# Moving the look at w2, the w2 slices and the third and fourth range of w1 in the plan of a two-layer GELU block

## The chip, the core and the metric

The kernel runs on one core of a Trainium2 chip. The metric is the device time in microseconds (us) of an execution. Engines are named as in the profile: PE (TensorE, the matrix products), PEld (its weight loads), DVE (VectorE), ACT (ScalarE), POOL (GpSimd) and SP (SyncE, which issues most transfers). Transfers between DRAM and the core go through 16 DMA engines.

## The reference

```
x: (8, 1024, 1024)   w1: (1024, 4096)   w2: (4096, 1024)      all float32
h = x @ w1
h = 0.5 * h * (1 + tanh(sqrt(2 / pi) * (h + 0.044715 * h ** 3)))
out = h @ w2
```

## The kernel before

All products run in float16 with float32 sums; x, w1 and w2 are scaled by their largest entries first. Both products are done by block schemes with fewer products than the plain one, whose left and right factors are sums of blocks that DVE makes beforehand.

**First product.** The rows of x come in 32 pairs k of two tiles of 128 rows, the columns of w1 in 4 ranges r (each of 512 columns in both halves of w1). One (k, r) is a quad: a Quad1 has seven block products m1 to m7 of four matmuls of 512 columns, in the psum banks pa, pb and pc; the first seven quads are Plain, with 32 matmuls. The list `order` fixes the sequence: the first 6 pairs with range 0, then 1, 2 and 3 (quads 0 to 23), then pairs 6 to 27 with all four ranges each (quads 24 to 111), then the last 4 pairs range by range. A range's factors are prepared while the range ahead of it is multiplied: eight loads (load_w1, L257, on POOL's queue for ranges 1 to 3), eight looks for the largest entry (look_w1, a DVE reduction, L143), widest_w1 (L268, and the `spread` at L148), scale_w1 (a matmul `rows` of 128x128 on PE at L153 that brings the largest to all partitions, read back at L156, with the scales at L273 and L274), eight casts to float16 (cast_w1, L166 on ACT, L168 on POOL, L170 on DVE), and four sums T1 to T4 of 128x2048 (sum_w1, on DVE, L159 and L162). Quad1 needs T2 at m6, T1 at m5, T3 at m7 and T4 at m4; m7 and m4 of a quad run in the next unit, m3 in the one behind that. The sums of x blocks (xs) are on DVE too, in four pieces a pair.

After a quad ACT copies pa (L455, L465, L474), DVE adds pb and pc to the copies (the e groups of L159), ACT takes the gelu (L406), POOL scales and casts (g, L168), and SP stores g to DRAM (gd, L411).

**w2.** While the middle quads run, w2 is read twice. The look: 32 tiles of 128x1024 (look_w2_load, L298, on SP), one reduction each on DVE (look_w2, the w2c group at L143), then widest_w2 and scale_w2. Then eight slices c: four loads (load_w2, L322, on SP), four casts (cast_w2, the wu groups, two on DVE at L170 and two on POOL at L168), 32 sums of 128x256 on DVE (sum_w2, wt), and stores of the sums to DRAM (wd, L344 and L347). In the last 16 quads they are fetched from there (L353).

**What sets the order.** It is written by hand: `plan(u, slot, f, ...)` puts a call into one of seven slots 0 to 6 of unit u, and `unit` writes the quad's products with `background(u, slot)` between them; `early(p, ...)` is slot p % 4 of unit p // 4. Each engine keeps the order in which the calls are written, so an instruction that waits holds up all that stand behind it on its engine, and a transfer that waits for a buffer all behind it in its queue. Loop `k` of x: load_x, look_x on ACT (junk, L181), cast_x on DVE, turn_x (a transposing transfer, L198, on SP), sum_x.

**Buffers.** wpool has 28 buffers of 4 KB a partition (w1 tiles, w1 factors, at first x tiles); k4 has 15 of the same size (x, xT, xs, look tiles, w2 tiles, wu, wt); a tile takes a free one, and its first writer waits for the last reader of the tile ahead of it.

Of the kernel before, what the change touches and what calls it, by code (L numbers as in the profile page):

```python
# [26 lines left out]
B11, T4, B21, B22, T1, T2, T3 = range(7)  # L27
# [48 lines left out]
def kernel(  # L76
# [18 lines left out]
    IK = I // P // 2  # L95
# [3 lines left out]
    FIRST = 6  # L99
# [6 lines left out]
    k4 = ctx.enter_context(tc.tile_pool(name="k4", bufs=15))  # L106
# [33 lines left out]
    V, S, G = nc.vector, nc.scalar, nc.gpsimd  # L140
# [436 lines left out]
    def plan(u, slot, f, *args):  # L577
        assert 0 <= u, (f, args)
        todo.setdefault((u, slot), []).append((f, args))
# [6 lines left out]
    def early(p, f, *args):  # L586
        plan(p // 4, p % 4, f, *args)

    for k in range(1, FIRST):
        for h in range(2):  # L590
            c = 2 * k + h
# [15 lines left out]
        early((3, 4, 6, 7, 8, 9, 10, 11)[n], load_w1, 1, n)  # L607
        early((7, 8, 10, 11, 12, 13, 14, 15)[n], look_w1, 1, n, True)
    early(15, widest_w1, 1)
    early(17, scale_w1, 1)  # L610
    early(17, factors, 0, FIRST, 1)
    for n in range(8):
        early(17 + n // 2, cast_w1, 1, n, (V, S, G, V, S, V, G, V)[n])
    for i, t in enumerate((T1, T3, T2, T4)):
        plan(*((5, 3), (FIRST, 0), (FIRST, 1), (FIRST + 1, 2))[i], sum_w1, 1, t)
    for r in range(2, NR):
        u = (r - 1) * FIRST
        for n in range(8):
            v = u - 1 + n // 2
            plan(v, 1 if v >= FIRST else 0, load_w1, r, n, *((k4, "k4") if r == 3 and n < 2 else ()))  # L620
            plan(v + 1, 3 + n % 2, look_w1, r, n, True)
        plan(u + 3, 4, widest_w1, r)
        plan(u + 4, 1, scale_w1, r)
        plan(u + 4, 1, factors, 0, FIRST, r)
        for n in range(8):
            v = u + 4 + n // 6
            plan(v, 3 + n % 4 * (n < 6), cast_w1, r, n, S if n % 2 else G)
        for i, t in enumerate((T1, T3, T2, T4)):
            plan(u + 5, 4 + i - i // 3, sum_w1, r, t)
    for i, t in enumerate((T1, T3, T2, T4)):  # L630
        plan(3 * FIRST + i, 5, sum_w1, 0, t)

    for k in list(middle) + list(last):
        a = at[k] if k in middle else at[last[0]]
        for h in range(2):
            c = 2 * k + h
# [9 lines left out]

    u = at[middle[0]] - 1
    for ic in range(2 * IK):
        plan(u + ic - 1, 3, look_w2_load, ic)
        plan(u + ic, 6, look_w2, ic)  # L650
    u += 2 * IK
    plan(u, 4, widest_w2)
    plan(u + 1, 1, scale_w2)
    stored = [max(i for i, o in enumerate(RIGHT_SUMS) if RIGHT_PLACE[o[0] - 16][0] == t) for t in range(3)]
    for c in range(8):
        v = u + 2 + c * 11 // 2
        for j in range(4):
            plan(*((v - 1, 1), (v - 1, 3), (v - 1, 6), (v, 1))[j], load_w2, c, j)
            plan(v, (1, 2, 4, 6)[j], cast_w2, c, j, G if j % 2 else V)
        for i in range(len(RIGHT_SUMS)):  # L660
            plan(*divmod(7 * (v + 1) + i, 7), sum_w2, c, i)
            for t in range(3):
                if i == stored[t]:
                    plan(*divmod(7 * (v + 1) + i + 2, 7), store_w2, c, t)
        for node in FORMS:
            if node < 16:
                plan(v + 2, 3, store_block, c, node)
    assert v + 6 < at[last[0]]
    for i, node in enumerate(FORMS):
        r, n = divmod(i, 7)  # L670
# [46 lines left out]
    with tc.manual_schedule(  # L717
# [14 lines left out]
        for c in range(2):  # L732
# [6 lines left out]
            t = x16[c]  # L739
# [63 lines left out]
```

## Time and profile before

| what | value |
|---|---|
| three runs, us | 1552.01, 1553.94, 1554.4 (median 1553.94) |
| profiled execution, us | 1554.94 |
| its span, us | 1552.9 |
| granted PE clock, mean | 1.0 |
| DMA busy share, 175 to 375 us; 380 to 650 us | 0.78; 0.88 |
| DVE busy, 175 to 375 us; 380 to 650 us | 131.39 us; 213.97 us |
| HBM read, written | 96.99 MB, 114.29 MB |

The profile's times run from the span's start. The page's busy line gives each engine's busy time, its share of the span and its instructions. In a list of waits, a line has who waited, for whom, the sum in us, how often, and the longest. In a timeline a line has start, length, engine, line of the kernel, operation, output and inputs, and in brackets how long the engine had been idle before and what ended that. In the chain of waits a piece has start, length and what it was.

The first product lasts to about 820 us of the span, the second from there to the end. Quad 12, the first with range 2, starts at 104.9 us, quad 18, the first with range 3, at 143.8, quad 24 at 181.4, and quad 57, where the first slice of w2 is cast, at 381.1.

### The profile page before, as it was taken

To read this page: it belongs to the slowest core of one execution; us is meant where nothing else is said; L and a number is where in the kernel's file an instruction comes from. 1 tells how busy PE (TensorE), PEld (TensorE's weight loads), DVE (VectorE), ACT (ScalarE), POOL (GpSimd) and SP (SyncE) were. 2 spreads that over 40 slices of the span, in tenths; PEclk is the share of its full clock that TensorE was granted. 3 is DMA by queue.
4 is the path that set the end of the run, shared out by engine and by line. 5 is a ranking of instruction groups with operands and counts; after the bars stand their busy time and mean duration, and the time that the engine had idled before them with its cause. 6 is when DMAs were issued, how large, how long until landed. Compare 5 with 4: busy or idle time off the path is not lost.

```text
span 1552.9 us, 28548 instructions
## 1 busy us (share of the span) xinstructions
PE 1523.7 (98%) x10415; PEld 1016.2 (65%) x10415; DVE 1176.9 (76%) x2361; ACT 726.0 (47%) x1281; POOL 448.6 (29%) x568
## 2 busy tenths in 40 slices
PE   7989999999999999999999999999999999999999
PEld 4434444444444444444447888888888888888888
DVE  6886666666788886765238888888888888888886
ACT  6567777777777777787662111111111111111111
POOL 2667544445565665554442000000000000000000
PEclk9999999999999999999999999999999999999999
DMA  8555778787897988983699677677668667776872
GB/s 322 179 175 185 207 232 256 219 253 209 256 275 234 277 257 238 278 241 116 195 249 263 121 151 140 137 132 159 130 125 158 141 134 135 154 135 120 164 140 79
DMA packets 459804, 293.91 MB, mean 189 GB/s; under 512 B 333840, under 2 KB 427024, under 8 KB 459664
## 3 DMA queue, kind: packets, MB, share of 16 engines
q1 hardware_dynamic: 456208, 279.52, 70.8%
q0 software_dynamic: 3456, 12.58, 2.5%
q8 instruction: 81, 1.33, 0.4%
q14 instruction: 59, 0.48, 0.1%
HBM read 96.99 MB, written 114.29 MB: 136 GB/s over the span
## 4 chain that ended last, share of the span: by engine, by line
PE 91%; DMA 3%; ACT 2%; DVE 2%; issue 1%; POOL 1%; SPq 0%; ACTq 0%; POOLq 0%; DVEq 0%
PE pa L359 48%; PE pc L359 29%; PE pb L359 13%; DMA wn<-in_w_dram 1%; DMA gd<-g 1%; ACT e L406 1%; DMA w<-wd 1%; ACT junk L181 1%; POOL g L168 0%; ACT w L166 0%; PE pb L371 0%; DVE w1c L143 0%; DVE e L159 0%; DVE w L162 0%; PE turned L207 0%
## 5 line engine op out<-in xcount | busy, mean ns | idle before, releaser
L168 POOL TENSOR_SCALAR g<-e,rs 128x512 f16<-128x512 f32 x512 | 400.3, 792 | 354.1 <-ACT e L406 279.7
L359 PEld LDWEIGHTS <-gs 128*128 128x128 f16 x4608 | 450.6, 98 | 56.0 <-DVE gs L162 1.6
L359 PEld LDWEIGHTS <-xs 128*128 128x128 f16 x1936 | 189.3, 98 | 238.2 <-issue 8.2
L159 DVE TENSOR_TENSOR e<-pc,e 128x512 f32<-128x512 f32 x242 | 160.7, 684 | 196.0 <-ACT e L474 195.3
L359 PEld LDWEIGHTS <-xT 128*128 128x128 f16 x1676 | 163.5, 98 | 195.2 <-DVE xT L214 0.4
L359 PE MATMUL pa<-w,gs 128*128 128x256 f16 x2304 | 288.3, 273 | 1.6 <-ACT e L406 1.0
L406 ACT ACTIVATE e<-e,us 128x512 f32<-128x512 f32 x363 | 250.6, 720 | 21.1 <-DVE e L159 20.8
L359 PE MATMUL pa<-w,xs 128*128 128x512 f16 x968 | 248.4, 379 | 8.9 <-ACT e L455 5.9
L359 PE MATMUL pa<-w,xT 128*128 128x512 f16 x1080 | 255.6, 379 | 0.2 <-DVE xT L214 0.2
L359 PE MATMUL pc<-w,xs 128*128 128x512 f16 x968 | 248.4, 379 | 0.0
L359 PEld LDWEIGHTS <-gT 128*128 128x128 f16 x2048 | 200.3, 98 | 23.7 <-DMA w<-wd 0.6
L528 ACT ACTIVATE o<-pa,vo 128x256 f32<-128x256 f32 x96 | 45.2, 471 | 336.1 <-PE pa L359 333.4
L359 PE MATMUL pc<-w,gs 128*128 128x256 f16 x1536 | 193.8, 273 | 0.3 <-DMA w<-wd 0.3
L359 PE MATMUL pa<-w,gT 128*128 128x256 f16 x1024 | 132.7, 273 | 0.3 <-DMA w<-wd 0.3
L359 PE MATMUL pb<-w,xT 128*128 128x512 f16 x484 | 124.2, 379 | 0.0
L524 DVE SCALAR_TENSOR_TENSOR o<-pc,vo,o 128x256 f32<-128x256 f32 x160 | 77.0, 481 | 58.7 <-PE pc L359 58.7
L465 ACT COPY e<-pa 128x512 f32<-128x512 f32 x121 | 70.8, 585 | 92.2 <-PE pa L359 88.6
L162 DVE TENSOR_TENSOR gs<-gT,gs 128x1024 f16<-128x1024 f16 x160 | 109.2, 682 | 1.2 <-DMA gT<-gd 0.5
L524 DVE SCALAR_TENSOR_TENSOR o<-pa,vo,o 128x256 f32<-128x256 f32 x192 | 91.9, 479 | 19.4 <-PE pa L359 19.1
L359 PE MATMUL pb<-w,gs 128*128 128x256 f16 x768 | 99.5, 273 | 0.3 <-DVE gs L162 0.3
L359 PE MATMUL pc<-w,gT 128*128 128x256 f16 x768 | 99.5, 273 | 0.0
L455 ACT COPY e<-pa 128x512 f32<-128x512 f32 x121 | 69.8, 577 | 45.8 <-PE pa L359 45.6
(84 smaller groups left out, 1355.7 us busy)
## 6 DMA issues: line engine op xcount, KB each, us to landing
gd<-g SPq DMA_DIRECT2D x484, 128.0 KB, 3.0
wn<-in_w_dram SPq DMA_DIRECT2D x72, 512.0 KB, 5.5
xn<-in_x_dram SPq DMA_DIRECT2D x64, 512.0 KB, 5.7
out_dram<-o SPq DMA_DIRECT2D x62, 512.0 KB, 3.3
w<-wd SPq DMA_DIRECT2D x25, 512.0 KB, 5.9
wn<-in_w_dram POOLq DMA_DIRECT2D x24, 512.0 KB, 5.8
wd<-wt SPq DMA_DIRECT2D x24, 512.0 KB, 4.9
gd<-g SPq DMA_DIRECT2D x14, 256.0 KB, 4.9
```

Source lines behind the costliest of these rows:

```text
L159: V.tensor_tensor(out=o, in0=a, in1=b, op=ALU.add)
L162: V.tensor_tensor(out=o, in0=a, in1=b, op=ALU.subtract)
L168: G.tensor_scalar(out=o, in0=i, scalar1=s, scalar2=1.0, op0=ALU.mult, op1=ALU.mult)
L181: S.activation(out=junk, in_=xraw[c], func=ACT.Abs, accum_out=xl[:, c:c + 1])
L359: nc.tensor.matmul(bank, lhsT=left(i), rhs=right[i], start=start and i == 0, stop=i == n - 1, skip_group_check=True,)
L406: S.activation(out=e, in_=src, func=ACT.Gelu_apprx_tanh, scale=self.u[half])
L455: S.copy(self.e11, self.pa)
L465: S.copy(self.e12, self.pa)
L524: V.scalar_tensor_tensor(out=o, in0=ps, scalar=v, in1=o, op0=ALU.mult, op1=ALU.add)
L528: S.activation(out=o, in_=ps, func=ACT.Copy, scale=v)
```

## The change

- Range 1: scale, factors and casts stand a quarter of a quad later (early 18 and on for 17 and on). T1 to T4 are made in the order T1, T2, T3, T4, at (6,0), (6,2), (7,1), (7,3), where T1, T3, T2, T4 stood at (5,3), (6,0), (6,1), (7,2).
- Ranges 2 and 3 (the third and fourth): u is one less, so all loads, looks, casts and the scale stand a quad sooner; widest stands in slot 5 instead of 4; the sums stand at (u+5, 4), (u+5, 6), (u+6, 1) and (u+6, 3) of the smaller u. All loads stand in slot 1, and the two of range 3 that used pool k4 use wpool.
- The look at w2: one tile every 35/8 slots (8 in 5 quads) instead of one a quad, each loaded 7 slots ahead of its look instead of 10. It ends in quad 42 instead of 54; widest_w2 stands in quad 43 instead of 55.
- The slices of w2: one every 7 quads, from quad 45 to 94, instead of every 5.5 from 57 to 95. The loads of slice v stand at (v-2,4), (v-2,6), (v-1,2), (v-1,4) instead of (v-1,1), (v-1,3), (v-1,6), (v,1); casts, sums and stores stand as before against v.

```diff
-    early(17, scale_w1, 1)
-    early(17, factors, 0, FIRST, 1)
+    early(18, scale_w1, 1)
+    early(18, factors, 0, FIRST, 1)
     for n in range(8):
-        early(17 + n // 2, cast_w1, 1, n, (V, S, G, V, S, V, G, V)[n])
-    for i, t in enumerate((T1, T3, T2, T4)):
-        plan(*((5, 3), (FIRST, 0), (FIRST, 1), (FIRST + 1, 2))[i], sum_w1, 1, t)
+        early(18 + n // 2, cast_w1, 1, n, (V, S, G, V, S, V, G, V)[n])
+    for i, t in enumerate((T1, T2, T3, T4)):
+        plan(FIRST + i // 2, (0, 2, 1, 3)[i], sum_w1, 1, t)
     for r in range(2, NR):
-        u = (r - 1) * FIRST
+        u = (r - 1) * FIRST - 1
         for n in range(8):
             v = u - 1 + n // 2
-            plan(v, 1 if v >= FIRST else 0, load_w1, r, n, *((k4, "k4") if r == 3 and n < 2 else ()))
+            plan(v, 1, load_w1, r, n)
             plan(v + 1, 3 + n % 2, look_w1, r, n, True)
-        plan(u + 3, 4, widest_w1, r)
+        plan(u + 3, 5, widest_w1, r)
         plan(u + 4, 1, scale_w1, r)
...
         for i, t in enumerate((T1, T3, T2, T4)):
-            plan(u + 5, 4 + i - i // 3, sum_w1, r, t)
+            plan(u + 5 + i // 2, (4, 6, 1, 3)[i], sum_w1, r, t)
...
     for ic in range(2 * IK):
-        plan(u + ic - 1, 3, look_w2_load, ic)
-        plan(u + ic, 6, look_w2, ic)
-    u += 2 * IK
+        t = 7 * u + ic * 35 // 8
+        plan(*divmod(t - 7, 7), look_w2_load, ic)
+        plan(*divmod(t, 7), look_w2, ic)
+    u += 20
...
     for c in range(8):
-        v = u + 2 + c * 11 // 2
+        v = u + 2 + c * 7
         for j in range(4):
-            plan(*((v - 1, 1), (v - 1, 3), (v - 1, 6), (v, 1))[j], load_w2, c, j)
+            plan(*((v - 2, 4), (v - 2, 6), (v - 1, 2), (v - 1, 4))[j], load_w2, c, j)
             plan(v, (1, 2, 4, 6)[j], cast_w2, c, j, G if j % 2 else V)
```

## The prediction

> **What bounds the kernel now.** I read the page first, then the waits of TensorE (PE), then the chain and the timelines around the longest of them. A quad below is a unit u, one (k, r) product: 28 products of 512 columns, 6.045 us when nothing waits (the chain repeats every 6.04 us from 150 to 380 us).
>
> ```profile
> PE 1523.7 (98%) x10415; PEld 1016.2 (65%) x10415; DVE 1176.9 (76%) x2361; ACT 726.0 (47%) x1281; POOL 448.6 (29%) x568
> ```
>
> PE is busy for 98%, so only its gaps can be gained, 29 us in all. 11.6 us of them lie in the first 40 us, 3.3 at the end, and 2.4 at 800 to 860 us, where the second product begins; the change touches none of these. The rest stands in three lines of the waits of PE:
>
> ```profile
> PE pa L359 <- ACT e L455: 5.9, 8, 2.0
> PE pa L359 <- DVE w L162: 3.0, 2, 1.8
> PE rows L153 <- DVE spread L148: 2.8, 2, 2.1
> ```
>
> So 11.7 us, with 0.2 us at an xT copy 11.9 us, is all that this change can touch. PE's timeline places it: 0.68 and 0.21 at 56 us (scale of range 1); then range 2 and range 3:
>
> ```profile
> 93.85 0.33 PE L153 MATMUL rows<-identity,spread 128*128 128x128 f32 x1 [2.13 <-DVE spread L148]
> ...
> 102.31 1.02 PE L359 MATMUL pa<-w,xs 128*128 128x512 f16 x4 [0.36 <-ACT e L455]
> ...
> 110.32 1.04 PE L359 MATMUL pa<-w,xs 128*128 128x512 f16 x4 [1.80 <-DVE w L162]
> ```
>
> Range 3 has 0.36 and 1.19 at 141 and 148 us, and no wait at its rows matmul. Between 380 and 650 us (w2's slices) there are six waits, 5.2 us, all for ACT's copy L455. The waits of VectorE (DVE) in that stretch, and the chain at 484 us, tell why:
>
> ```profile
> DVE wu L170 <- DMA wn<-in_w_dram: 20.1, 9, 4.4
> ```
> ```profile
> 484.58 5.49 DMA wn<-in_w_dram
> ...
> 490.10 0.76 DVE wu L170
> ...
> 491.24 0.61 DVE e L159
> ...
> 494.95 1.11 ACT junk L181 x2
> 496.07 0.48 ACT e L455
> ...
> 496.59 1.02 PE pa L359 x4
> ```
>
> A w2 tile lands late, the cast L170 holds up DVE, the add behind it comes late, ACT waits for the add with its gelu, and the copy that frees PE's bank comes last. Waits of DVE of 3.27, 3.65, 3.73 and 4.44 us cost PE 0.3 to 2.05 us; shorter ones cost nothing.
>
> **w2's slices (gain).** No work is removed; 32 loads and 40 stores of SP's queue are moved. Before, a slice's four loads stand 7, 6, 5 and 5 slots ahead of their casts (7 slots a quad, 0.86 us each: 6.0 to 4.3 us), and the landing view gives 4.0/5.8/8.4 us (least, median, most) for line 322. After, they stand 11, 10, 9 and 9 slots ahead, 9.5 to 7.8 us: each gains 3.4 us or more. That covers the 3.27 wholly and leaves 0.3 to 1.0 of the other three, under what PE feels. Slices every 7 quads in place of 5.5 also thin out the 32 sums on DVE (0.2 us each) and 3.6 MB of DMA a slice, which ran at a DMA share of 0.88 from 380 to 650 us. In SP's queue the loads pass the g stores and a transpose; in the changed program's order (counted in PE's products) the buffers they take were last read 10 to 28 us earlier, where before four loads took a buffer freed less than 6 us earlier, so SP stops less. Residue 0.6 (between none and 1.7): **-4.6 us** (-5.2 to -3.5).
>
> **Looks at w2.** 32 looks of 1.14 us (L143), in 20 quads in place of 32: DVE gets 0.7 us more a quad, and its busy time from 175 to 375 us is 131 of 200 us, so that lies beside PE. The load stands 7 slots ahead and not 10, 2.6 us less. Before, looks began 7.7 to 10.5 us after the issue, so now 5.1 to 7.9, against 3.7/4.1/6.9 us to landing: a wait of up to 1.8 us at the worst, below the 3 us from which PE felt one. Queued behind a waiting look are the adds L159, and behind these ACT's gelu and copy. Nearest rows: 0 PE waits from 150 to 380 us. **0** (0 to +1).
>
> **Range 1 of w1, a quarter quad later.** The rows matmul no longer stands ahead of the third product of quad 4, but that product waits for the xT copy (L214, ends 56.8) behind look, spread and copy on DVE, which do not move. So the 0.9 us stays, and the rows matmul (0.2) no longer hides in it. Its sums come just in time: T3 is needed at 79.5 us and is ready at 78.2 by the shortest rows, 79.7 by the long ones. **+0.2** (0 to +0.5).
>
> **Range 2, a quad sooner (the step that I doubt).** 8 loads on POOL's queue (0.75 us each), 8 looks, widest, spread, rows, 8 casts, 4 sums move up. From 63.24 to 93.72 us DVE works without a break (30.4 busy of 30.5 us), and the spread is the end of that work. The changed order of DVE's instructions up to the spread has three xs pieces less (0.34, 0.49, 0.34), three adds of 0.6 less, one cast of 0.69 more: 30.5 - 1.2 - 1.8 + 0.7 = 28.2 us. So the spread is ready at 63.4 + 28.2 = 91.6 us, 2 us sooner; but PE wants it a whole quad sooner, behind m7 of quad 9, at 85.51 + 0.2 = 85.7. **The wait does not go, it grows from 2.13 to as much as 5.9 us.** With each row at its shortest the work of 30.5 us would be 25.4, because sums that take 1.13 us stand in the trace at up to 2.2 where POOL's casts run beside them; by the same rows the new order takes 23.2, and with a third of the drag 25.5, a wait of 3.2. I take 4.6, nearer the middle: +2.5. Then the sums of range 2 (10,4) to (11,3) are a quad ahead of quad 12, and the 1.80 goes: -1.8. ACT's batch of three casts (0.36) moves along unchanged. **+0.7** (-0.7 to +2.0).
>
> The Trainium skill (SBUF — State Buffer, "SBUF: two separate sides") says that VectorE with two SBUF inputs and GpSimd lock a shared port pair for a whole instruction; the trace agrees (the sum of 2048 at 1.13 alone, 2.2 beside POOL's). By that rule alone the drag would follow POOL's casts, which stay, and the wait would be nearer 5.9 than 3.2.
>
> **Range 3, a quad sooner.** Nothing else fills DVE from quad 11 to 14: looks 2.3 and adds 1.9 of 6 us. Its spread stood ready at 132.3 for a rows matmul at 132.77; the relative slots stay. The 1.19 of T2 goes, 0.36 stays. The two tiles that leave pool k4 for wpool take slots freed long before. **-1.2** (-1.55 to -0.8).
>
> **Sum.** -4.6 + 0 + 0.2 + 0.7 - 1.2 = -4.9 us. The profiled execution took 1554.94 us (span 1552.9 and 2.0 around it), so 1550.0; it lies 1.0 above the median of the runs, 1553.94, so **1549.0** against that median. 0.2% (3.1 us) is about what a measurement of this kernel can tell from no change.
>
> **Rivals.**
> *The wall at quad 9 eats the gain.* The wait is 5.9 us (+3.8 instead of +2.5), T3 is late by 0.3, and the clock falls after so long a gap. For the last: the start has a PE gap of 4.53 us, and the 30 warm-up products behind it take 5.58 us, 16 later ones 1.91 (0.11 each): 2.1 us lost. The longest gap later on is 2.13, with the granted clock at 1.00. So +1.3 + 0.3 + 2.1, 1552.7 us. The Trainium skill (TensorE: Matmul & The Clock Gate, "What's actually happening") puts the fall to half clock after an idle window of about 3.4 us; an estimate from that page is a loss of 1.7 us, 1550.7 with nothing else. Within 0.2%; chance 0.18.
> *w2's waits were not the lead.* SP lags by the g stores (the second slice's first load went out 6.6 us after its slot), so an earlier slot gives no earlier issue; half of the 4.6 stays: 1551.3. Against it: POOL's casts, for which SP waits, are themselves behind late w2 tiles. 0.10.
> *Looks become the bound, slower.* The stretch moves 232 GB/s, 1.40 MB a quad; 0.6 looks more make 1.72 MB, at the 277 GB/s of the densest 40 us slice 6.2 us a quad, over 6.045: 20 x 0.17 = 3.4 us. Around each of five x loads (2 of 512 KB) landings then pass the 3 us of slack, 1.6 us each, 8 us: 1560.4. It decides from landings of about 8 us, and only one in the present 32 reached 6.9. 0.10.
>
> **Chances.** Forecast 0.62, rivals 0.18, 0.10, 0.10. The first two rivals fall within 0.2%: faster 0.62, same 0.28, slower 0.10. The range goes from the best ends (-5.2 - 0.7 - 1.5 = -7.4, 1546.5) to the first rival, 1553.0; the last is left out.
>
> **What would show it.** w2: no DVE wait for wn over 2 us from 330 to 650 us, and at most 0.6 us of PE waits there. Looks: w2c from 181 to some 300 us, no PE wait. Range 2: a PE wait for the spread of 3.2 to 5.9 us near 86 us, none for w L162. Range 3: no w L162 wait. Wrong would be a short wait at quad 9 (DVE less bound than I sum up), or PE waits among the looks.

## The result and the profile after

The changed kernel takes 1555.59 us (median of 20 runs, 1552.82 to 1560.09), the kernel before 1553.05 (20 runs, 1550.72 to 1556.36) beside it: ratio 1.0015, 95% interval 1.0008 to 1.0022, or +1.2 to +3.4 us. That is within 0.2%, and on the other side of no change than the forecast of 1549.0; the time lies above the range, which ended at 1553.0. The profiled execution took 1556.61 us (span 1554.8), 1.7 more than the one of before.

The page's busy line of the changed kernel, then four of PE's waits (who waited, for whom, sum, times, longest):

```profile
PE 1525.8 (98%) x10415; PEld 1016.7 (65%) x10415; DVE 1179.2 (76%) x2361; ACT 724.2 (47%) x1281; POOL 456.4 (29%) x568
```
```profile
PE rows L153 <- DVE spread L148: 4.3, 2, 3.9
PE pa L359 <- ACT e L455: 3.7, 5, 1.7
PE pa L359 <- DVE xT L214: 1.1, 1, 1.1
...
PE pa L359 <- ACT xT L212: 0.9, 1, 0.9
```

The waits that the change aimed at are smaller: 3.7 us for L455 where there were 5.9, and none for w L162. But PE is busy for 2.1 us *more* with the same 10415 instructions: they ran slower. The timeline of PE around quad 9 and the windows there (us, busy time of PE, PEld, DVE, ACT, POOL, then granted clock, DMA share, GB/s) show where:

```profile
85.47 1.03 PE L359 MATMUL pa<-w,xs 128*128 128x512 f16 x4
90.42 0.48 PE L153 MATMUL rows<-identity,spread 128*128 128x128 f32 x1 [3.92 <-DVE spread L148]
90.69 1.91 PE L359 MATMUL pc<-w,xs 128*128 128x512 f16 x4
92.39 1.91 PE L359 MATMUL pb<-w,xT 128*128 128x512 f16 x4
94.10 1.91 PE L359 MATMUL pa<-w,xs 128*128 128x512 f16 x4
95.81 1.09 PE L359 MATMUL pc<-w,xs 128*128 128x512 f16 x4
```
```profile
88.00:90.00 2.00, 0.00 (x0) 0.00 (x0) 2.00 (x5) 0.66 (x2) 1.56 (x2) 0.77 0.24 81
90.00:92.00 2.00, 1.58 (x5) 0.70 (x6) 1.78 (x8) 0.00 (x0) 0.30 (x1) 0.50 0.34 116
...
94.00:96.00 2.00, 2.00 (x6) 0.76 (x5) 1.81 (x5) 0.00 (x0) 0.00 (x0) 0.52 0.00 0
96.00:98.00 2.00, 2.00 (x11) 0.88 (x9) 0.11 (x1) 1.89 (x4) 0.60 (x1) 1.00 0.00 0
```

Range 2's rows matmul now stands at quad 9 and waits 3.92 us (forecast 4.6, bounds 3.2 to 5.9). Behind it the clock is at half until 96 us: three groups of four products take 1.91 us in place of 1.03. That is some 2.6 us, nearly the 2.1 of the first rival, and not in the forecast.

Two other things are new. At the sums of range 2 a wait of 1.07 us (at 114.9 us) stands where 1.80 stood. And among the looks, which had cost PE nothing, there is one of 1.69 us at 256 us and one of 0.37 at 310. The timeline of the changed kernel there, first SP's queue, then the engines:

```profile
241.76 2.78 SPq L198 DMA_TRANSPOSE xT<-x  x1
244.64 1.21 SPq L411 DMA_DIRECT2D gd<-g  x2
245.91 1.50 SPq L298 DMA_DIRECT2D wn<-in_w_dram  x1
```
```profile
252.29 1.22 DVE L143 TENSOR_REDUCE w2c<-wn 128x1 f32<-128x1024 f32 x1 [3.92 <-DMA wn<-in_w_dram]
...
254.14 0.72 ACT L406 ACTIVATE e<-e,us 128x512 f32<-128x512 f32 x1 [3.29 <-DVE e L159]
254.77 1.04 ACT L181 ACTIVATE junk<-xn 128x1024 bf16<-128x1024 f32 x1
...
255.81 0.56 ACT L455 COPY e<-pa 128x512 f32<-128x512 f32 x1
...
256.43 1.02 PE L359 MATMUL pa<-w,xs 128*128 128x512 f16 x4 [1.69 <-ACT e L455]
```

The issue of a transpose holds SP for 2.78 us (the median of its 52 issues is 1.24), the look's load goes out behind it, VectorE stands 3.92 us at the look, ACT's gelu waits for the add behind the look, and PE for the copy that stands behind the gelu and ACT's look at x (L181). It is the chain that the forecast had read at the slices, now at the looks. Of the six gaps of 5.2 us at the slices none is left. By this one execution: slices -5.2, range 3 -1.2, looks +2.1, range 1 +1.1, range 2 +1.1 and the clock +2.6, the start of the second product (waits for transfers of w) +1.4; together +1.9, and the span grew by 1.9.

### The profile page after: what moved, and what is told of

It reads as the page before. It is cut to its first block, busy times and chain, and to the rows that moved or that the text cites. A ratio compares the mean times of both kernels' runs of the same rounds, so it can differ in the third digit from the quotient of the medians.

```text
span 1554.8 us, 28528 instructions
## 1 busy us (share of the span) xinstructions
PE 1525.8 (98%) x10415; PEld 1016.7 (65%) x10415; DVE 1179.2 (76%) x2361; ACT 724.2 (47%) x1281; POOL 456.4 (29%) x568
## 3 DMA queue, kind: packets, MB, share of 16 engines
q8 instruction: 81, 1.33, 0.3%
## 4 chain that ended last, share of the span: by engine, by line
PE 92%; DMA 3%; DVE 3%; ACT 1%; issue 1%; POOL 1%; SPq 0%; ACTq 0%; DVEq 0%; POOLq 0%
PE pa L359 49%; PE pc L359 29%; PE pb L359 13%; DMA gd<-g 1%; DMA w<-wd 1%; DMA wn<-in_w_dram 1%; DVE w1c L143 1%; DVE e L159 0%; PE pb L371 0%; DVE w L162 0%; POOL g L168 0%; DVE xs L162 0%; ACT e L406 0%; PE turned L207 0%; ACT junk L181 0%
## 5 line engine op out<-in xcount | busy, mean ns | idle before, releaser
L168 POOL TENSOR_SCALAR g<-e,rs 128x512 f16<-128x512 f32 x512 | 405.5, 803 | 368.3 <-ACT e L406 290.8
L162 DVE TENSOR_TENSOR gs<-gT,gs 128x1024 f16<-128x1024 f16 x160 | 109.7, 686 | 1.0 <-POOL g L168 0.5
L524 DVE SCALAR_TENSOR_TENSOR o<-pa,vo,o 128x256 f32<-128x256 f32 x192 | 92.1, 480 | 20.3 <-PE pa L359 20.1
L455 ACT COPY e<-pa 128x512 f32<-128x512 f32 x121 | 69.8, 577 | 48.3 <-PE pa L359 47.5
```

The costliest lines, as they stand in the source:

```text
L162: V.tensor_tensor(out=o, in0=a, in1=b, op=ALU.subtract)
L168: G.tensor_scalar(out=o, in0=i, scalar1=s, scalar2=1.0, op0=ALU.mult, op1=ALU.mult)
L455: S.copy(self.e11, self.pa)
L524: V.scalar_tensor_tensor(out=o, in0=ps, scalar=v, in1=o, op0=ALU.mult, op1=ALU.add)
```

## The experiments

Ratios are to the kernel before, measured between the runs of each (5 in e11, 8 to 12 in the others); "us" is the ratio less 1, times the median of the kernel before, good to about 1.6 us either way, so a difference of two of them to about 2. "Clock" is the mean granted clock over a kernel's timed runs (in the kernel before 0.9994 to 0.9996); 0.001 of it is 1.55 us. The single executions agree: in the 188 of these kernels and the changed one, an execution took 1.5 us longer for each 0.001 that its clock lay lower than in others of the same kernel (standard error 0.14).

| run | what | ratio, 95% | us | clock |
|---|---|---|---|---|
| e1 | w1 part alone | 0.9997, 0.9986 to 1.0009 | -0.5 | 0.9984 |
| e2 | w2 part alone | 0.9996, 0.9986 to 1.0006 | -0.6 | 0.9993 |
| e3 | range 2 back | 1.0009, 0.9999 to 1.0020 | +1.4 | 0.9981 |
| e4 | ranges 1 and 2 back | 1.0014, 1.0003 to 1.0025 | +2.2 | 0.9982 |
| e5 | w2 part, looks loaded sooner | 0.9974, 0.9965 to 0.9983 | -4.0 | 0.9995 |
| e6 | changed, idle products | 1.0017, 1.0006 to 1.0027 | +2.6 | 0.9993 |
| e7 | changed, half looks at range 2 | 0.9987, 0.9974 to 0.9999 | -2.0 | 0.9994 |
| e8 | changed, looks loaded sooner | 0.9992, 0.9982 to 1.0001 | -1.2 | 0.9985 |
| e9 | e8 with idle products | 0.9975, 0.9965 to 0.9986 | -3.9 | 0.9998 |
| e10 | e5, slices' loads at the old lead | 0.9986, 0.9975 to 0.9996 | -2.2 | 0.9993 |
| e11 | e5, one cast moved to VectorE | 0.9947, 0.9935 to 0.9959 | -8.2 | 0.9996 |
| e12 | looks alone, loaded sooner | 0.9998, 0.9987 to 1.0009 | -0.3 | 0.9987 |
| f1 | e8 again | 0.9986, 0.9976 to 0.9995 | -2.2 | 0.9986 |
| f2 | e9 again | 0.9976, 0.9967 to 0.9985 | -3.7 | 0.9996 |
| f3 | e8, half the idle products | 0.9969, 0.9959 to 0.9979 | -4.8 | 0.9998 |
| f4 | e6 again | 1.0017, 1.0007 to 1.0026 | +2.6 | 0.9994 |

The first four shared one chip, e5 to e8 a second, e9 to e12 a third, f1 to f4 the second again.

### The parts by themselves: e1 to e4

e1, against the changed kernel:

```diff
-        t = 7 * u + ic * 35 // 8
-        plan(*divmod(t - 7, 7), look_w2_load, ic)
-        plan(*divmod(t, 7), look_w2, ic)
-    u += 20
+        plan(u + ic - 1, 3, look_w2_load, ic)
+        plan(u + ic, 6, look_w2, ic)
+    u += 2 * IK
...
-        v = u + 2 + c * 7
+        v = u + 2 + c * 11 // 2
...
-            plan(*((v - 2, 4), (v - 2, 6), (v - 1, 2), (v - 1, 4))[j], load_w2, c, j)
+            plan(*((v - 1, 1), (v - 1, 3), (v - 1, 6), (v, 1))[j], load_w2, c, j)
```

> The changed kernel with its w2 part (looks and slices) as in the kernel before: only ranges 1 to 3 of w1 are moved. Theory A (the price lies in range 2: PE waits 3.9 us for the spread at quad 9, the granted clock falls to 0.50 for some 6 us behind it, which costs 2.6 us, and a new wait of 1.07 us comes at quad 13; range 1 costs 1.1, range 3 gains 1.2): +3.6 us against the kernel before, with the gap at 86 us and the fallen clock at 90 to 96 us in its profile. Theory B (w2's denser looks and the start of the second product cost what w2's slices gain; the w1 part is what I forecast, -0.3): between -1 and +1 us.

e2 is the kernel before with these lines the other way round.

> The changed kernel with its w1 part as in the kernel before: only w2's looks and slices are moved. Theory A: the six gaps of 5.2 us among the slices go, the looks give one wait of up to 2 us: -3 to -5 us against the kernel before, no granted clock below 0.9 near 90 us. Theory B: +1 to +2.5 us, as the changed kernel.

e3 and e4, against the changed kernel: range 2 gets the loop body that the kernel before has, range 3 keeps the new one; in e4 range 1 has the old lines too.

```diff
-    for r in range(2, NR):
-        u = (r - 1) * FIRST - 1
+    for r in range(2, 3):
+        u = (r - 1) * FIRST
...
+    for r in range(3, 4):
+        u = (r - 1) * FIRST - 1
```

> The changed kernel with range 2 alone back at the slots it has in the kernel before. Theory A: the wait for the spread is 2.1 us again and not 3.9, the clock stays at 1.00 there, the 1.8 us wait for T2 comes back: 3.7 us under the changed kernel, so -1 to -3 us against the kernel before. Theory B: no more than 1 us under the changed kernel.

> As the run before it, with range 1 back as well; range 3 and w2 stay changed. Theory A: a further 1.1 us (the two waits of 0.86 and 1.15 us at 52 and 58 us become 0.9 again), so -3 to -4.5 us against the kernel before, the fastest of the four. Theory B: as the run before it, within 0.5 us, since range 1's wait is for an xT copy that does not move.

Neither theory stands. e1 has the gap of 3.92 us and the fallen clock in its profile, as theory A said, but a time of -0.5 and not +3.6. e2 gained 0.6 where A said 3 to 5, though the gaps at the slices are gone from its profile; it has 2.10 and 0.37 us at the looks. And e3 and e4 did not get the price back. PE's waits in e4 tell why, with VectorE's timeline in e3:

```profile
PE pa L359 <- DVE w L162: 4.0, 1, 4.0
```
```profile
103.40 1.21 DVE L143 TENSOR_REDUCE w1c<-wn 128x1 f32<-128x1024 f32 x1
104.53 1.57 DVE L162 TENSOR_TENSOR w<-w 128x2048 f16<-128x2048 f16 x1
106.03 1.21 DVE L143 TENSOR_REDUCE w1c<-wn 128x1 f32<-128x1024 f32 x1
107.16 5.69 DVE L162 TENSOR_TENSOR w<-w 128x2048 f16<-128x2048 f16 x3
```

With range 2 back, two looks at range 3 (w1c), a quad sooner, stand between its sums (w, L162) on VectorE: PE's wait for T2 goes from 1.80 to 4.0 us. The moves of the two ranges hang together, so these runs put one long gap in the place of another and could not price range 2. The clock's records are instructive. The gap of 4.0 us is followed by half clock in e4 (0.50 from 112 to 118 us) and by full clock in e3; a gap of 2.13 us, the same as in the kernel before, is followed by half clock in e4:

```profile
92.00:94.00 2.00, 0.63 (x4) 0.39 (x5) 1.93 (x5) 1.06 (x2) 1.46 (x2) 1.00 0.00 1
94.00:96.00 2.00, 2.00 (x8) 0.81 (x7) 1.93 (x8) 0.00 (x0) 1.96 (x4) 0.67 0.50 141
96.00:98.00 2.00, 2.00 (x7) 0.66 (x5) 2.00 (x1) 0.19 (x1) 1.81 (x2) 0.50 0.87 291
```

So the same gap brings a fall in one execution and none in another (the section on the clock shows when), and the mean clock of the timed runs says more than one profile.

### The looks: e5 and e8

The loads of the looks move 4 slots up, in e5 in the kernel e2, in e8 in the changed kernel:

```diff
-        plan(*divmod(t - 7, 7), look_w2_load, ic)
+        plan(*divmod(t - 11, 7), look_w2_load, ic)
```

> The w2 part alone (w1 as in the kernel before), with each look's load 11 slots ahead of its look in place of 7. Theory C (the looks cost: every fourth quad x's loads and a transpose stand in the queue ahead of a look's load, the look waits 3.4 to 4.8 us for it on VectorE, and PE waits 2.1 us once): VectorE's waits for wn between 190 and 300 us fall under 1.5 us each, the PE gap of 2.10 us goes, and the time falls by about 2 us, to 2 to 4 us under the kernel before. Theory D (8 looks in 5 quads are too many for the DMA engines, however early they are loaded): waits of 3 us or more stay.

> The changed kernel with the looks' loads 11 slots ahead in place of 7 and nothing else changed. Theory C: the gap of 1.69 us at 256 us goes, about 2 us under the changed kernel, so level with the kernel before (within 1 us); what is then left against the first run of these four is the w1 part, some 2 us. Theory D: as the changed kernel, 1 to 2.5 us over the kernel before.

Theory C holds, with a larger size than the 2 us expected: e5 is 3.4 us under e2, e8 3.6 us under the changed kernel. PE's own waits between 190 and 320 us say the same: 2.3 to 4.4 us, 3.4 on average, in the seven profiles of kernels with looks 8 in 5 quads and loads 7 slots ahead, and none in the nine with 11. The 2.1 read in the changed kernel was at the low end. VectorE's waits from 190 to 300 us, the changed kernel first, then e5, where no line for wn is left:

```profile
DVE w2c L143 <- DMA wn<-in_w_dram: 24.6, 10, 4.6
```
```profile
DVE e L159 <- ACT e L474: 22.7, 16, 3.0
```

VectorE stood idle about as long in both, but in e5 behind PE's own pace (waiting for ACT's copies), in the changed kernel behind a load, with the adds held up. PE has no gap from 149 to 800 us in e5. The transfers were not too many (theory D): the same 8 in 5 quads cost PE no wait once they were issued in time. They are slower than before, though; issues from 175 to 330 us (count, size, median us to landing) of the kernel before and of the changed one:

```profile
wn<-in_w_dram SPq DMA_DIRECT2D x26, 512.0 KB, 4.1
```
```profile
wn<-in_w_dram SPq DMA_DIRECT2D x35, 512.0 KB, 5.4
```

### VectorE's wall at quad 9: e7

```diff
-        absmax(w1c[:, r, n:n + 1], wraw[r, n].rearrange("p c n -> p (c n)"))
+        absmax(w1c[:, r, n:n + 1], wraw[r, n][:, 0] if r == 2 else wraw[r, n].rearrange("p c n -> p (c n)"))
```

> The changed kernel, whose eight looks at range 2 of w1 read half of each tile; the other half goes unlooked at, so the scale of that range comes from half of its values. Theory F (at quad 9 VectorE's work sets the end: 28.2 us of it from 63 us on): 8 x 0.55 = 4.4 us less work, the wait for the spread falls from 3.9 to under 0.5 us, and the clock stays at 1.00. If the wait is for a late load of w1 or for POOL instead, it stays above 2 us.

Theory F is right as to what bounded it, and too large in size: the wait for the spread fell from 3.92 to 1.38 us, not under 0.5. With 0.68 us a look in place of 1.21, VectorE catches up with the loads of w1:

```profile
84.81 0.69 DVE L143 TENSOR_REDUCE w1c<-wn 128x1 f32<-128x512 f32 x1 [0.69 <-DMA wn<-in_w_dram]
...
86.55 0.69 DVE L143 TENSOR_REDUCE w1c<-wn 128x1 f32<-128x512 f32 x1 [0.72 <-DMA wn<-in_w_dram]
```

These two waits are 1.41 us, about what is left of PE's wait. The mean clock was back at 0.9994, and the time 4.3 us under the changed kernel's: some 2.5 from the gap, the rest about what 0.0009 of the clock is worth (1.4).

### The clock: e6, e9 and f1 to f4

e6, against the changed kernel; e9 and f2 have the same in e8, f3 with 7 for 14:

```diff
+    def fill(n):
+        b = bank("pb")
+        for _ in range(n):
+            nc.tensor.matmul(
+                b, lhsT=identity16, rhs=w1set[1, B11][:, 0, :],
+                start=True, stop=True, skip_group_check=True,
+            )
...
+        if r == 2:
+            plan(u + 4, 1, fill, 14)
         plan(u + 4, 1, scale_w1, r)
```

> The changed kernel with 14 products that nothing reads (512 columns each, some 3.6 us) put between the third product of quad 9 and the rows matmul of range 2; they stand where PE waits 3.9 us. Theory E (the fall of the clock is a cost of its own, set off by the length of the gap): the rows matmul starts at the same time as in the changed kernel, the gap is under 0.5 us, the granted clock stays at 1.00 from 88 to 96 us, mean clock of the runs 0.9995 in place of 0.9985, and the time is 1.5 to 2.6 us under the changed kernel's. If the clock has no part in it: as the changed kernel, 1 to 2.5 us over the kernel before.

> The changed kernel with the looks' loads 11 slots ahead (as the run that was 0.9 us under the kernel before, with a mean granted clock of 0.99845) and the 14 idle products at quad 9 as well. Theory E (the clock's fall costs 1.6 us a run on average, 0.001 of 1553 us, in about half of which the idle products help, and does not depend on the looks): mean clock 0.9993 or more, and 1 to 1.6 us less than without them, so 2 to 2.5 us under the kernel before. If the clock's fall is without a price in the end time: as without them, 0.5 to 1.5 us under.

> The changed kernel with the looks' loads 11 slots ahead, on one chip with the three runs after it. Theory E (the fall of the clock costs 1.6 us a run on average): mean clock 0.9985, 1 to 1.5 us under the kernel before.

> The run before it with the 14 idle products at quad 9. Theory E: mean clock 0.9995 or more, and 1 to 2 us under the run before it. If the idle products' gain was chance: the same time within 0.7 us.

> As the run before it with 7 idle products: a gap of some 2.4 us is left at quad 9. If the length of the gap sets off the fall, mean clock and time are nearer to those with 14 (a gap of 2.1 us in the kernel before leaves 0.9995); if any gap there does, nearer to those without.

> The changed kernel with the 14 idle products and the looks' loads 7 slots ahead, as in its first run, which was 2.3 us over the kernel before at a mean clock of 0.99925. Theory E with the looks at 3.5 us: 3 to 4 us over the second run of these four, that is about level with the kernel before to 1 us over. If it is again 2 us or more over: the looks cost more when the clock is kept up, and the two prices do not add.

Fourteen idle products take 3.0 us, not the 3.6 expected, and start and stop within the old gap: in every profile with 14 of them 0.90 us of it is left and the clock stays up at quad 9, as in e9's windows:

```profile
90.00:92.00 2.00, 1.15 (x6) 0.31 (x4) 1.96 (x6) 0.29 (x1) 1.33 (x2) 1.00 0.39 131
92.00:94.00 2.00, 1.95 (x10) 0.99 (x11) 1.93 (x8) 0.00 (x0) 0.72 (x1) 1.00 0.19 66
```

Without the looks' waits theory E holds: f2 is 1.5 us under f1 and f3 2.6 under it on the same chip, with clocks of 0.9996 and 0.9998 against 0.9986 (e8 to e9, on two chips, 2.7). Each of the three is good to about 2 us only, but all go one way, and 0.0010 to 0.0012 of the clock is 1.6 to 1.9. The traces show the price without the noise of the runs: from the rows matmul at quad 9 to the gap of 1.07 us at the sums of range 2, PE took 24.50 us in f1 (from 89.28) and 21.77 in f2 (from 89.27), 2.7 us less. In e8, whose fall was shorter, it took 23.32, so 1.5 to 1.6 more than in f2.

What decides whether the clock falls can be read from windows of 0.05 us. A fall lasts 3.41 us (e8, e9, e10, e12, f3, the first in e4, and one in e5 at 840 us) or 6.83 (the changed kernel, e1, f1, the second in e4), and falls of one execution start a whole number of such steps apart: e4's two 17.06 us, five steps, f1's and one at the very end of its span 1460.9 us, 428 steps of 3.413. So cut each trace into steps of 3.413 us, counted from its fall. In the step just ahead of each of these eleven falls PE is idle for 2.09 us or more. No other step of these ten traces, from 22 to 1540 us, has over 1.94 us of idle time. The gaps of 2.13 us in e5 and e12 that brought no fall are cut in two by the end of a step, with at most 1.13 us in either.

By these traces a gap brings a fall when about 2 us of it lie within one step, and where the steps lie differs from execution to execution. That makes a gap of 3.92 us an almost certain fall (four of four profiles with it) and one of 2.0 to 2.5 us an occasional one (5 of 17). Seven products that cut the gap to 2.41 us did as well as fourteen on average, although the clock fell in f3's own profiled execution (0.50 from 92 to 94 us). In e9's the clock fell at 58 us, behind a wait for xT of 2.24 us that the idle products do not touch.

With the looks' waits in place the idle products gained nothing, twice (e6, f4: +2.6 each, where the changed kernel has +2.3). f4 is 6.4 us over f2, where the changed kernel is 3.6 to 4.5 over e8 and f1. There the two prices do not add, although in e7, with the looks' waits in place and the clock up, they did. Why stays open; the profiles of e6 and f4 show 4.0 and 3.8 us of PE's waits between 250 and 310 us, that of the changed kernel 2.1, but e7's shows 4.4.

### Where the slices' gain comes from, and a faster kernel: e10, e12, e11

e10, against e5, gives the slices' loads their old places; e12 also the old spacing:

```diff
-            plan(*((v - 2, 4), (v - 2, 6), (v - 1, 2), (v - 1, 4))[j], load_w2, c, j)
+            plan(*((v - 1, 1), (v - 1, 3), (v - 1, 6), (v, 1))[j], load_w2, c, j)
```

> The w2 part with looks loaded 11 slots ahead (3.5 us under the kernel before), but each slice's loads as close ahead of their casts as in the kernel before (7 to 5 slots), at the new spacing of 7 quads. Theory G (the loads' lead frees the slices, as I forecast): the 3 to 5 us of PE gaps between 390 and 650 us come back, VectorE's waits of 3 us and more for wn with them, and the time is within 1 us of the kernel before. Theory H (the thinner spacing alone frees the DMA engines): no gap there, and 3 us under the kernel before.

> The kernel before with 8 looks in 5 quads, loaded 11 slots ahead; slices every 5.5 quads with their loads as in the kernel before, w1 as before. Theory: denser looks that are loaded early enough cost and gain nothing by themselves: within 1 us of the kernel before, with the gaps of the slices (3 to 5 us) in the profile, some 100 us earlier. If the slices now meet other traffic, their gaps change and the time with them, by up to 2 us either way.

e12 is where it was expected, at -0.3, with a gap at the slices in its profile (2.50 us, where 3 to 5 was expected). So the slices' part is worth the 3.7 us between e12 and e5. Some of that is clock: behind e12's gap it fell to 0.50 (at 426 us), and its mean is some 0.0007 under e5's, 1.1 us. e10 fits theory H on PE, with no gap at the slices and an interval of -3.9 to -0.6 us that holds the 3 expected; on VectorE waits of over 3 us are left, as in theory G. Its waits of VectorE from 380 to 700 us, and below them those of e5:

```profile
DVE wu L170 <- DMA wn<-in_w_dram: 9.0, 5, 3.4
```
```profile
DVE wu L170 <- DMA wn<-in_w_dram: 4.9, 2, 2.7
```

In both the slices begin before 380 us; from 310 us on the waits are 11.9 us in e10 and 4.9 in e5. At the old lead VectorE still waits, up to 3.4 us, but at the new spacing PE has no gap there. The kernel before waited 20.1 us so, and lost 5.2 on PE. So the lead shortens VectorE's waits; that the spacing gives it room to catch up behind a late tile is the likely reason for PE, but no run shows the lead alone at the old spacing. By the ratios each brings about half (1.9 us between e12 and e10, 1.8 between e10 and e5); the intervals are too wide to tell the shares.

e11, against e5:

```diff
-            plan(v, 3 + n % 4 * (n < 6), cast_w1, r, n, S if n % 2 else G)
+            at6 = (u + 4, 6) if n == 6 else (v, 3 + n % 4 * (n < 6))
+            plan(*at6, cast_w1, r, n, V if n == 6 else S if n % 2 else G)
```

> The w2 part with looks loaded 11 slots ahead, w1 as in the kernel before but for one thing: for ranges 2 and 3 the seventh of the eight casts, GpSimd's last (1.1 to 2.1 us, for which the sums wait 1.6 and 1.0 us on VectorE), is done by VectorE one slot ahead of its place, where VectorE stands idle for 4.0 and 5.5 us. If the wait for T2 is set by that cast and not by VectorE's amount of work: the sums start 1.0 to 1.5 us sooner, the gaps of 1.82 and 1.20 us at 110 and 148 us shrink to 0.5 or less together, and the time is 2 us less, 5 to 6 us under the kernel before. If not: 3.5 us under, gaps as they were.

It is the fastest of all, 8.2 us (0.41% to 0.65%, five runs) under the kernel before, where 5 to 6 was expected, and 4.2 under e5 by the ratios. Of these, 3.0 are the two gaps; the rest is within what the ratios can tell. VectorE's timeline in e11:

```profile
98.58 1.10 DVE L170 TENSOR_SCALAR w<-wn,w1i 128x1024 f16<-128x1024 f32 x1
102.66 1.29 DVE L159 TENSOR_TENSOR e<-pc,e 128x512 f32<-128x512 f32 x2 [2.97 <-ACT e L474]
103.86 0.68 DVE L159 TENSOR_TENSOR e<-pb,e 128x512 f32<-128x512 f32 x1
104.46 5.10 DVE L162 TENSOR_TENSOR w<-w 128x2048 f16<-128x2048 f16 x4
```

The cast lies where VectorE stood idle, the four sums run in one piece from 104.46 to 109.56 us (in e5 they ended at 111.78), and PE's waits for w L162, 3.0 us in the kernel before, are gone from its list. The moves of ranges 2 and 3 were after the same 3.0 us; one cast in each range gets them without a new wait.

## Why the prediction was wrong, point by point

- **w2's slices, -4.6: right in size and in the mechanism on PE.** No gap is left, and e5 against e12 gives -3.7. VectorE's waits for a tile fell from 20.1 to 3.7 us (330 to 650 us), the longest to 2.2. The share put on the lead is not shown: with the spacing alone, named beside it, PE had no gap there (e10).
- **Looks, 0 (0 to +1): this step failed.** It cost 3.4 to 4.5 us (e2 to e5, the changed kernel to e8 and f1). The "wait of up to 1.8 us at the worst" took the lead that the issues had had before and took 2.6 us off. But that lead holds only while SP's queue keeps its slots. About every fourth quad SP waits there for a cast of x (five waits, 11.9 us, up to 3.0, between 175 and 330 us) and is held by the issue of the transposes (2.78 us in the lines above), ahead of a look's load, and the denser landings went from 4.1 to 5.4 us. VectorE's five longest waits were 3.1 to 4.6 us. The 3 us from which PE felt a wait at the slices was no threshold either: in the changed kernel's profile one of the five, of 3.92 us, cost PE 1.69, and one of 4.56 cost it no more than 0.2. The place, SP's queue, was named for the slices and left out for the looks.
- **Range 1, +0.2: about right.** PE's wait for xT is 1.1 to 1.2 us in nine of the eleven profiles with range 1 moved (2.24 in e7 and e9), in place of 0.9, so +0.3. The 0.86 at 52 us that makes it +1.1 in the changed kernel's profile stands in kernels with range 1 as before too (e10 0.44, e12 1.71). No run moved range 1 alone.
- **Range 2, +0.7: right.** The wait of 3.92 lies within the bounds, the 1.80 went, though 1.07 took its place. The work sum on VectorE as its reason was borne out: VectorE worked without a break from 64.07 us to the spread's end at 90.37, 26.3 us, between the 23.2 and 28.2 of the sum, and in e7 less work cut the wait.
- **The clock, 0 in the sum: the second step that failed.** Put into a rival at 2.1 and 0.18, for a wait of 5.9 us, it costs 1.5 to 2.7 us. The longest gap with full clock behind it had been 2.13 us, the prediction itself read 2.1 us lost behind 4.53 us at the start, and the wait was forecast at 4.6, so the profile gave no ground to expect the clock to hold. With the clock kept up, e9 and f2 stand within 0.3 us of e5: the rest of the w1 part is near the -0.3 forecast.
- **Range 3, -1.2: right** in the profile; it hangs on range 2 being moved as well (e3, e4).
- **The third rival**, the looks as the bound, had the right place and the wrong mechanism. It needed the DMA engines to be too slow, and priced 11.4 us (3.4 and 8); e5 shows that it was the moment of issue.

With the slices at -3.7, the looks at +3.4 to +4.5, the rest of the w1 part at +0.2 and the clock at +1.5 to +2.7 the sum is +1.4 to +3.7, and +2.3 was measured. That is no separate proof, since the terms are differences along one chain of kernels from the kernel before to the changed one; what backs them are the waits and the clock in the traces. By itself the w1 part measured -0.5 (e1), less than its share here, which the intervals of 1.7 us each allow but do not explain.

On the clock the Trainium skill (TensorE: Matmul & The Clock Gate, "What's actually happening") has the clock at half after an idle window of about 3.4 us, and has the windows run freely, not started anew by a kernel. The half clock agrees (0.50 in the windows), and so do the windows: falls of 3.41 and 6.83 us, and two in e4 that start five times 3.41 apart. That the whole window is idle is not needed: 2.09 to 2.50 us of it were enough in e4, e5, e9, e10, e12 and f3, and the measurement decides.

## What to carry to other kernels

Where loads are made denser, take the lead from the issue that comes last in the queue's cycle, not from the median landing, and make the lead longer, not shorter; here four slots were worth as much as the whole gain at the slices. Treat a predicted PE gap of 2 us or more as a chance of 3.4 or 6.8 us at half clock, growing with the gap, and put that into the forecast. Before moving a block of work sooner to meet a deadline, look for the one instruction on the slowest engine that the deadline hangs on.

## What was not expected of the hardware

The granted clock fell to 0.50 behind gaps of 2.13 (e4, e10), 2.24 (e9), 2.41 (f3) and 2.50 us (e12), for 3.41 us each, and did not fall behind one of 4.01 us (e3); the same gap of 2.13 us left it at 1.00 in the profiles of the kernel before, e2, e5, e11 and e12. e3's trace has no fall from which its steps could be counted, so its gap is not explained. Where VectorE's sums of 128x2048 ran beside GpSimd's casts of g, the two did not share the cost alike: in e11 the four sums took 1.28 us each on average, and GpSimd's four casts beside them 1.33 each (5.32 us together from 106.13 us), where one alone takes 0.69. In the changed kernel, at 73.25 us, a sum beside such casts took 2.29.
